# Two sums of weights made by transfers, and the tensor engine held in program order through the mixer's attention stage

## The chip, the cores and the metric

The kernel runs on one core of a Trainium2 chip. The metric is the device time of one execution in microseconds (us). The time before is 1540.34 us, the median of 3 runs (1540.05 to 1541.54). A profile is one execution, recorded instruction by instruction on the engines PE (matmul), DVE (vector), ACT (scalar), POOL (GpSimd) and SP (which only issues transfers).

## What is computed

Two layers of a decoder trunk on 512 tokens of width 1024, in float32. Each layer has three sub-layers with a norm before and after:

```python
def reference(x, mem, positions, rel_bias, ...):
    for l in range(DEPTH):                                   # 2
        a = hybrid_mixer(rms_norm(x, pre_mix_g[l]), ...)     # 8 latent heads and 8 dilated heads, one output projection
        x = x + rms_norm(a, post_mix_g[l])
        c = memory_cross_attention(rms_norm(x, pre_xattn_g[l]), rms_norm(mem, mem_g[l]), ...)   # 4 heads, 256 memory tokens
        x = x + rms_norm(c, post_xattn_g[l])
        hdn = jnp.square(jax.nn.relu(rms_norm(x, pre_mlp_g[l]) @ w_up[l]))      # width 4096
        x = x + rms_norm(hdn @ w_down[l], post_mlp_g[l])
    return x
```

In the mixer one input projection `w_in` gives the latent columns (query rank 384, key-value rank 256, 32 rotary) and the dilated heads' q, k, v. The latent heads get their queries and keys through a second, normalised projection. The dilated heads use a shared relative bias.

## The kernel before

**Precision.** Each float32 operand is split into a high and a low part, and each product is three matmuls: low by high, high by low, high by high (`mm`, L234, its matmuls at L240 to L242). Weights arrive by SP's queue in a `raw` buffer (8 of them, `raw_w`, L151); ACT writes the high part `whi` and DVE the low part `wlo` (`parts_w`, L161, without a gain; `load_w`, L168, with a gain per row at L192 and L198). There are five buffers each for high and low parts, and one comes free when PE has done the last product with it.

**Order.** A planner orders each engine's queue when the program is built: it goes by program order, and lifts an instruction ahead of others where, by its own model of times, its inputs are there and theirs are not. Two calls limit it. `tc.keep_in_program_order(ins)` keeps a PE instruction behind the PE instruction before it in the program. `tc.issue_after(ins)` queues what is in its block behind `ins` on that engine. Before the change the first call is used for transposes of some stages (`transpose`, L224, while `in_turn[0]` is set), the second for a few weight conversions.

**The mixer's stages.** First the dilated heads' v, q and k are projected (15 to 85.6 us in layer 0). `ev_kd` (L637) evicts each tile of k from PSUM: ACT writes `kh` (L642), DVE `kl` (L646), and POOL copies both to the other half of the partitions (L648). Then comes the attention stage (85.6 to 270.6 us in layer 0, 848.6 to 1027.4 in layer 1). `weave` takes steps in turn from the generator `attention()` and, as filling, from `latent()` (the latent projection, `ptm` with outputs `cq` and `ckv`; its transposes `ctp`; the second projections `pkn`, `pvm`; the queries' transposes `qtp`) and then `memory()` (the cross-attention's keys and values of the memory tokens: `pfm`, `ptm`). `attention()` makes for each of 16 heads four blocks of scores (`scores`, matmul `sp` at L470; DVE adds the bias and reduces at L474; ACT takes the exponential at L477; POOL normalises at L479), then for the head before it three groups of transposes (`ptp`, evicted by ACT at L498 and by DVE at L496), and for each pair of heads the weighted values (`op`, L231).

**PSUM.** There are four buffers of the products (`mm`), two of scores (`s`) and two of transposes (`t`). So the third score block of a head waits until DVE has read the first, and the third group of transposes until ACT has read the first.

**The MLP's second half.** The product with `w_down` is made in four quarters of the hidden width, each by seven products of half-size blocks instead of eight. The sums that these need are made on the activations in `left_forms` (L1018), and on the weights, in two groups g, in `right_form` (L1041) by DVE in place in the `raw` buffers: L1046 for product p = 5, L1048 for 6, L1050 for 7, L1052 for 4. `finish` (in the loop of products) adds each product into `acc` (L1120). After the last quarter, `done` (L1055) takes the sum of squares of a half row block (L373, the squares themselves go to a `junk` tile in SBUF), multiplies by the gain `gb` (L1058), and `add_post_norm` (L418) computes the scale (DVE `pnm` L421, POOL power `pnr` L139) and adds to the residual `xs` (L424). In layer 1 that result is transferred out; in layer 0 `norm_x` (L394) normalises it for the next layer (POOL L409 and ACT L406), and `transposed` makes the next layer's `xth` and `xtl`.

Of the kernel before, what the change touches and what calls it, by code (L numbers as in the profile page):

```python
# [45 lines left out]
def block_kernel(ctx: ExitStack, tc, x, mem, positions, rel_bias, w_in, q_norm_g, w_uq, kv_norm_g,  # L46
# [121 lines left out]
    def load_w(src, r0, kts, c0, width, gcol=None, heads=0):  # L168


        raw = raw_w(src, r0, kts, c0, width)
        hi = wp.tile([128, 2, 512], WD, tag="hi", name="whi")
        lo = wp.tile([128, 2, 512], WD, tag="lo", name="wlo") if SPLIT else None

        def cols(w, k, swap):
            v = w[:, k, :width]
            if not heads:
                return v
            if swap:
                return v.rearrange("p (h e c) -> p e h c", h=heads, e=2)  # L180
            return v.rearrange("p (e h c) -> p e h c", h=heads, e=2)

        if gcol is None and SPLIT:
            nc.scalar.activation(hi[:, :kts, :width], raw[:, :kts, :width], AF.Copy)  # L184
            nc.vector.tensor_sub(lo[:, :kts, :width], raw[:, :kts, :width], hi[:, :kts, :width].bitcast(F32))  # L185
            return hi, lo
        for k in range(kts):
            g = 1.0 if gcol is None else gT[:, gcol + k:gcol + k + 1]
            loads[0] += 1

            with tc.issue_after(token_parts[0]) if 3 <= loads[0] <= 8 else nullcontext():
# [31 lines left out]

    def transpose(out_, in_, ident_):  # L224
        ins = nc.tensor.transpose(out_, in_, ident_)  # L225
        if in_turn[0]:
            tc.keep_in_program_order(ins)
        clk[0] += 0.108

    def mm32(ps, lhsT, rhs, start, stop, rate=1.0):  # L230
        nc.tensor.matmul(ps, lhsT=lhsT, rhs=rhs, start=start, stop=stop)  # L231
        clk[0] += rhs.shape[-1] * 0.00167 * rate

    def mm(ps, lh, ll, rh, rl, first, last, more=False):  # L234
# [5 lines left out]
        nc.tensor.matmul(ps, lhsT=lh, rhs=rl, start=first, stop=False, skip_group_check=more)  # L240
        nc.tensor.matmul(ps, lhsT=ll, rhs=rh, start=False, stop=False, skip_group_check=more)  # L241
        nc.tensor.matmul(ps, lhsT=lh, rhs=rh, start=False, stop=last, skip_group_check=more)  # L242
# [127 lines left out]
    def sumsq(src, ss, scale=1.0):  # L370
        w = src.shape[-1]
        junk = unit("junk", (128, w))
        nc.scalar.activation(junk, src, AF.Square, scale=scale, accum_out=ss)  # L373
# [83 lines left out]
    behind = [None]  # L457

# [3 lines left out]
    def scores(P, parts, tb, scale):  # L462
# [3 lines left out]
        for i in range(NT):  # L466
            L = 128 * (i + 1)
            sp = pss.tile([128, 512], F32, tag="s", name="sp")
            for n, (q, k) in enumerate(parts):
                nc.tensor.matmul(sp[:, :L], lhsT=q[:, i * 128:(i + 1) * 128], rhs=k[:, :L],  # L470
                                 start=n == 0, stop=n == len(parts) - 1)
# [5 lines left out]
            nc.scalar.activation(Pi, Pi, AF.Exp, bias=nm[:, i:i + 1], scale=-1.0, accum_out=rs[:, i:i + 1])  # L477
# [89 lines left out]
    for l in range(DEPTH):  # L567
# [50 lines left out]
        def ev_ckv(t, ps):  # L618
            ckv[t] = unit("ckv")
# [17 lines left out]
        def ev_kd(m, ps):  # L637

            for a in range(2):
                here, there = slice(a * 64, a * 64 + 64), slice(64 - a * 64, 128 - a * 64)  # L640
                u = unit("kh", dt=WD)
                nc.scalar.activation(u[here, :], ps[here, :], AF.Copy)  # L642
# [240 lines left out]

        weave(attention(), [latent_gen, memory()], lambda: RATIOS[0] if not scored[0] else RATIOS[1])
        OTh = [o[0] for o in outs]
# [132 lines left out]
        def left_forms(F, ra, rb):  # L1018
# [11 lines left out]
            nc.vector.tensor_add(s1, a21, a22)  # L1030
            part(5, s1)
            nc.vector.tensor_sub(s2, s1, a11)
# [4 lines left out]
            nc.vector.tensor_sub(a12, a12, s2)  # L1037
# [3 lines left out]
        def right_form(p, b):  # L1041
# [3 lines left out]
            if p == 5:  # L1045
                nc.vector.tensor_sub(b11, b12, b11)  # L1046
            elif p == 6:
                nc.vector.tensor_sub(b11, b22, b11)  # L1048
            elif p == 7:
                nc.vector.tensor_sub(b12, b22, b12)  # L1050
            elif p == 4:
                nc.vector.tensor_sub(b11, b21, b11)  # L1052
            return parts_w({1: b11, 5: b11, 6: b11, 2: b21, 7: b12, 3: b22, 4: b11}[p])

        def done(t, n):  # L1055

            sumsq(acc[t][n], ss[t][:, n:n + 1], scale=1.0 / 32.0)
            nc.vector.tensor_mul(acc[t][n], acc[t][n], gb[n])  # L1058
            ready_halves[t] += 1
            if ready_halves[t] < 2:  # L1060
                return
# [7 lines left out]
        for qd_ in range(4):  # L1069
# [33 lines left out]
            for p, ps, first, last, dsts in plan:  # L1103
# [9 lines left out]
                def finish(j):  # L1113
                    for d, n in dsts:
                        t = d + j
                        if acc[t][n] is None:
                            acc[t][n] = unit("acc")
                            nc.vector.tensor_copy(acc[t][n], ps[j])  # L1118
                        else:
                            nc.vector.tensor_add(acc[t][n], ps[j], acc[t][n])  # L1120
                        if end and p in (2, 3, 4) or end and p == 7 and n == 1:
                            done(t, n)
# [9 lines left out]
                for g in range(2):  # L1132
                    w = right_form(p, B[g])
# [3 lines left out]
                if end and p == 7:  # L1137
                    last_w = [right_form(4, B[g]) for g in range(2)]
# [45 lines left out]
```

## Time and profile before

| | us |
|---|---|
| median of 3 runs | 1540.34 |
| runs from, to | 1540.05, 1541.54 |
| profiled execution, device time | 1542.4 |
| profiled execution, span | 1540.6 |
| PE busy in the span | 1504.2 |
| DVE, ACT, POOL busy in the span | 996.6, 820.6, 240.2 |

The span runs from the first to the last instruction of the profiled execution; that execution's device time is 1.8 us longer. In a timeline each row is a start, a duration, engine, line, operation, the tiles written and read, the shape, and in brackets the idle time before it with what ended it. Consecutive matmuls overlap in their modelled durations, so the pitch from start to start tells more than the duration. [...]

### The profile page before, as it was taken

Reading aid. Unit: us, or ns where it says so; the run is one execution under the profiler, and the core shown is the slowest. Engines: PE = TensorE matmul, PEld = TensorE weight load, DVE = VectorE, ACT = ScalarE, POOL = GpSimd, SP = SyncE. Lnnn points to the kernel's source line nnn. Section 1 sums busy time; section 2 is a strip of 40 time slices with the busy share of each in tenths; the row PEclk is TensorE's granted clock in tenths of the full one; section 3 lists DMA queues with packets and bytes.
Section 4 is the critical chain, followed back from the end, with each engine's and each line's share of the span. In section 5 each row is a group of like instructions: output and inputs, shape, how many; then the busy total and the mean of one; then the engine's idle time right before and its main releaser. Section 6 shows DMA issues by size and latency. Waiting matters only on the chain.

```text
span 1540.6 us, 21293 instructions
## 1 busy us (share of the span) xinstructions
PE 1504.2 (98%) x7861; PEld 1262.7 (82%) x7861; DVE 996.6 (65%) x1780; ACT 820.6 (53%) x1578; POOL 240.2 (16%) x429
## 2 busy tenths in 40 slices
PE   8999999999999999999989999999999999999996
PEld 6778788898898888888878877978988988888885
DVE  4556766456458668685974666654554695958678
ACT  5365666346456464544553666654454654546363
POOL 2053721021020000000012445201111100000001
PEclk9999999999999999999999999999999999999999
DMA  6423223513131505151542331253322324060612
GB/s 226 161 75 112 82 76 102 193 56 123 55 110 56 178 28 178 41 165 61 171 137 68 117 108 58 69 168 120 109 83 69 124 75 144 25 195 14 192 55 82
DMA packets 87404, 164.09 MB, mean 107 GB/s; under 512 B 6230, under 2 KB 12036, under 8 KB 87300
## 3 DMA queue, kind: packets, MB, share of 16 engines
q1 hardware_dynamic: 86724, 161.68, 32.3%
q8 instruction: 62, 1.02, 0.3%
q10 hardware_dynamic: 576, 1.05, 0.2%
q14 instruction: 42, 0.34, 0.1%
HBM read 154.29 MB, written 11.03 MB: 107 GB/s over the span
## 4 chain that ended last, share of the span: by engine, by line
PE 81%; DVE 8%; issue 6%; ACT 3%; POOL 1%; DMA 1%; SPq 0%; POOLq 0%; DVEq 0%; ACTq 0%
PE pfm L241 11%; PE pfm L240 11%; PE pfm L242 11%; PE ptm L240 6%; PE ptm L241 6%; PE ptm L242 6%; PE wa L240 3%; PE wa L242 3%; PE wa L241 3%; PE sp L470 3%; PE op L231 3%; PE ptp L225 2%; DVE wlo L198 2%; PE wc L240 2%; PE wc L242 2%
## 5 line engine op out<-in xcount | busy, mean ns | idle before, releaser
L241 PE MATMUL pfm<-xth,wlo 128*128 128x512 f32 (+1 forms) x896 | 322.4, 360 | 0.6
L240 PE MATMUL pfm<-xtl,whi 128*128 128x512 f32 (+1 forms) x896 | 322.2, 360 | 0.0
L242 PE MATMUL pfm<-xth,whi 128*128 128x512 f32 (+1 forms) x896 | 321.6, 359 | 0.0
L198 DVE SCALAR_TENSOR_TENSOR wlo<-raw,gT,whi 128x512 fp32r<-128x512 f32 (+3 forms) x332 | 229.6, 729 | 140.3 <-ACT whi L192 138.7
L192 ACT ACTIVATE whi<-raw,gT 128x512 fp32r<-128x512 f32 (+2 forms) x324 | 209.5, 697 | 187.6 <-PE pfm L242 100.3
L164 ACT ACTIVATE whi<-raw 128x1024 fp32r<-128x1024 f32 x112 | 118.1, 1060 | 143.0 <-PE pfm L242 52.8
L241 PEld LDWEIGHTS pfm<-xth,wlo 128*128 128x128 f32 x896 | 169.2, 189 | 27.2 <-DVE wlo L198 1.4
L242 PEld LDWEIGHTS pfm<-xth,whi 128*128 128x128 f32 x896 | 169.2, 189 | 25.5 <-issue 0.5
L240 PEld LDWEIGHTS pfm<-xtl,whi 128*128 128x128 f32 x896 | 169.2, 189 | 24.7
L165 DVE TENSOR_TENSOR wlo<-raw,whi 128x1024 fp32r<-128x1024 f32 x112 | 134.9, 1219 | 34.3 <-ACT whi L164 34.3
L139 POOL TENSOR_TENSOR pnr<-pnm,mhalf 128x1 f32<-128x1 f32 x24 | 18.0, 750 | 828.7 <-DVE pnm L421 828.6
L479 POOL TENSOR_SCALAR P<-P,rs 128x128 f32<-128x128 f32 (+3 forms) x128 | 72.0, 568 | 150.8 <-PE sp L470 66.3
L240 PE MATMUL wa<-wlo,fh 128*128 128x512 f32 x240 | 93.6, 390 | 0.5 <-DVE acc L1118 0.5
L241 PE MATMUL wa<-whi,fl 128*128 128x512 f32 x240 | 93.4, 389 | 0.0
L242 PE MATMUL wa<-whi,fh 128*128 128x512 f32 x240 | 93.4, 389 | 0.0
L477 ACT ACTIVATE P<-P,nm 128x128 f32<-128x128 f32 (+3 forms) x128 | 71.3, 558 | 23.4 <-DVE nm L474 22.8
L185 DVE TENSOR_TENSOR wlo<-raw,whi 128x1024 fp32r<-128x1024 f32 x32 | 39.1, 1222 | 59.3 <-ACT whi L184 58.6
L240 PE MATMUL ptm<-wlo,xth 128*128 128x512 f32 (+2 forms) x192 | 70.0, 365 | 3.9 <-DVE wlo L198 3.5
L184 ACT ACTIVATE whi<-raw 128x1024 fp32r<-128x1024 f32 x32 | 33.9, 1061 | 67.3 <-PE ptm L242 64.5
L241 PE MATMUL ptm<-whi,xtl 128*128 128x512 f32 (+2 forms) x192 | 67.7, 352 | 0.1
L242 PE MATMUL ptm<-whi,xth 128*128 128x512 f32 (+2 forms) x192 | 67.0, 350 | 0.0
L240 PEld LDWEIGHTS wa<-wlo,fh 128*128 128x128 f32 x240 | 45.0, 188 | 10.6 <-DVE acc L1118 1.4
(249 smaller groups left out, 3273.6 us busy)
## 6 DMA issues: line engine op xcount, KB each, us to landing
raw<-in_w_up SPq DMA_DIRECT2D x64, 512.0 KB, 4.6
raw<-in_w_down SPq DMA_DIRECT2D x64, 512.0 KB, 4.4
raw<-in_w_in SPq DMA_DIRECT2D x24, 512.0 KB, 5.7
raw<-in_w_xk SPq DMA_DIRECT2D x16, 512.0 KB, 4.4
raw<-in_w_xv SPq DMA_DIRECT2D x16, 512.0 KB, 3.7
raw<-in_w_mix_out SPq DMA_DIRECT2D x16, 512.0 KB, 4.4
raw<-in_w_xq SPq DMA_DIRECT2D x16, 512.0 KB, 5.4
raw<-in_w_xo SPq DMA_DIRECT2D x16, 512.0 KB, 3.5
```

The lines of the kernel that those rows point to most:

```text
L164: nc.scalar.activation(hi, raw, AF.Copy)
L165: nc.vector.tensor_sub(lo, raw, hi.bitcast(F32))
L185: nc.vector.tensor_sub(lo[:, :kts, :width], raw[:, :kts, :width], hi[:, :kts, :width].bitcast(F32))
L192: weight_parts[:] = [nc.scalar.activation(cols(hi, k, False), cols(raw, k, True), AF.Copy, scale=g).ins]
L198: nc.vector.scalar_tensor_tensor(lv, rv, g, hv, op0=OP.mult, op1=OP.subtract)
L231: nc.tensor.matmul(ps, lhsT=lhsT, rhs=rhs, start=start, stop=stop)
L240: nc.tensor.matmul(ps, lhsT=lh, rhs=rl, start=first, stop=False, skip_group_check=more)
L241: nc.tensor.matmul(ps, lhsT=ll, rhs=rh, start=False, stop=False, skip_group_check=more)
L242: nc.tensor.matmul(ps, lhsT=lh, rhs=rh, start=False, stop=last, skip_group_check=more)
L470: nc.tensor.matmul(sp[:, :L], lhsT=q[:, i * 128:(i + 1) * 128], rhs=k[:, :L], start=n == 0, stop=n == len(parts) - 1)
L477: nc.scalar.activation(Pi, Pi, AF.Exp, bias=nm[:, i:i + 1], scale=-1.0, accum_out=rs[:, i:i + 1])
L479: nc.gpsimd.tensor_scalar(Pi, Pi, rs[:, i:i + 1], 1.0, op0=OP.mult, op1=OP.mult)
```

## The change

Five edits, most of them in the two places named above.

1. The conversions of chunks 1 to 3 of the first latent load on ACT (rows `r0` not 0) are queued behind the third k tile's second `kh` eviction (`behind_keys`), until the first `ckv` is evicted. In the attention stage the first exponential of each head is queued behind the last `kh` eviction (`last_key`).
2. While `pinned` is set, which is through the whole `weave` of the attention stage in both layers, each PE matmul and transpose is kept in program order (`in_order`).
3. The sums of activations and weights change sign, so that all sums of weights are additions. In the last quarter of each layer the sums for p = 4 and p = 7 are no longer made by DVE: a transfer issued by GpSimd reads the second block from memory and adds it into the buffer (4 of 512 KB per layer, 8 in all). `finish` turns the sign of one half of the columns.
4. The junk squares of `done` go to a PSUM buffer of the pool `t`, but for p = 2.
5. In layer 1 the first two token tiles are finished by `finish_by_transfer`: DVE computes `acc` times scale times `gb` in one step, GpSimd issues a transfer that adds the residual from memory (4 of 256 KB), and SP transfers the result out. Their residual is no longer loaded.

```diff
-            with tc.issue_after(token_parts[0]) if 3 <= loads[0] <= 8 else nullcontext():
+            after = token_parts[0] if 3 <= loads[0] <= 8 else behind_keys[0] if r0 else None
+            with nullcontext() if after is None else tc.issue_after(after):
                 weight_parts[:] = [nc.scalar.activation(cols(hi, k, False), cols(raw, k, True), AF.Copy, scale=g).ins]
...
+    def in_order(ins):
+        if pinned[0]:
+            tc.keep_in_program_order(ins)
+
     def transpose(out_, in_, ident_):
         ins = nc.tensor.transpose(out_, in_, ident_)
         if in_turn[0]:
             tc.keep_in_program_order(ins)
+        else:
+            in_order(ins)
...
-        nc.tensor.matmul(ps, lhsT=lh, rhs=rl, start=first, stop=False, skip_group_check=more)
+        in_order(nc.tensor.matmul(ps, lhsT=lh, rhs=rl, start=first, stop=False, skip_group_check=more))
...
-            nc.scalar.activation(Pi, Pi, AF.Exp, bias=nm[:, i:i + 1], scale=-1.0, accum_out=rs[:, i:i + 1])
+            with tc.issue_after(last_key[0]) if pinned[0] and i == 0 else nullcontext():
+                nc.scalar.activation(Pi, Pi, AF.Exp, bias=nm[:, i:i + 1], scale=-1.0, accum_out=rs[:, i:i + 1])
...
-                nc.scalar.activation(u[here, :], ps[here, :], AF.Copy)
+                last_key[0] = nc.scalar.activation(u[here, :], ps[here, :], AF.Copy).ins
+                if m == 2 and a == 1:
+                    behind_keys[0] = last_key[0]
...
+        pinned[0] = True
         weave(attention(), [latent_gen, memory()], lambda: RATIOS[0] if not scored[0] else RATIOS[1])
+        pinned[0] = False
...
-            if p == 5:
-                nc.vector.tensor_sub(b11, b12, b11)
...
+            tile_, more, at = {1: (b11, None, None), 5: (b11, b12, None), 6: (b11, b22, None), 4: (b11, b21, (1, 0)),
+                               2: (b21, None, None), 7: (b12, b22, (1, 1)), 3: (b22, None, None)}[p]
+            if more is not None and at and qd_ == 3:
+                r0, c0 = qd_ * 1024 + g * 512 + at[0] * 256, at[1] * 512
+                nc.gpsimd.dma_start(tile_, w_down[l][r0:r0 + 256, c0:c0 + 512].rearrange("(k p) c -> p k c", p=128),
+                                    accum_op=OP.add)
+            elif more is not None:
+                nc.vector.tensor_add(tile_, tile_, more)
+            return parts_w(tile_)
+
+        def finish_by_transfer(t):
+            m = small("pnm", 1)
+            nc.vector.scalar_tensor_tensor(m, ss[t][:, 0:1], EPS, ss[t][:, 1:2], op0=OP.add, op1=OP.add)
+            r = rpow(m, "pn")
+            for n in range(2):
+                rows, cols = slice(t * 128, (t + 1) * 128), slice(n * 512, (n + 1) * 512)
+                nc.vector.scalar_tensor_tensor(acc[t][n], acc[t][n], r[:, 0:1], gb[n], op0=OP.mult, op1=OP.mult)
+                nc.gpsimd.dma_start(acc[t][n], xmid[rows, cols], accum_op=OP.add)
+                nc.sync.dma_start(out[0, rows, cols], acc[t][n])
...
-                            done(t, n)
+                            done(t, n, None if p == 2 else t_ps("junkp"))
...
-                        load_x(t, xmid)
+                        if l < DEPTH - 1 or t >= 2:
+                            load_x(t, xmid)
```

## Rows read from the trace of the kernel before

**Rows 1.** The page: busy time and instructions, and the granted clock by slice.
```profile
PE 1504.2 (98%) x7861; PEld 1262.7 (82%) x7861; DVE 996.6 (65%) x1780; ACT 820.6 (53%) x1578; POOL 240.2 (16%) x429
PEclk9999999999999999999999999999999999999999
```
**Rows 2.** Windows by stage: window, length, busy us of each engine, clock, DMA.
```profile
85.60:270.60 185.00, 176.05 (x1121) 147.58 (x1121) 123.48 (x349) 120.18 (x290) 77.15 (x148) 0.99 0.28 93
270.60:760.00 489.40, 488.83 (x2424) 413.96 (x2423) 319.23 (x442) 248.33 (x418) 31.21 (x48) 1.00 0.33 105
760.00:790.00 30.00, 25.79 (x110) 20.28 (x109) 27.75 (x48) 22.86 (x50) 9.58 (x12) 0.89 0.67 216
848.60:1027.40 178.80, 173.41 (x1121) 145.96 (x1121) 119.89 (x343) 115.66 (x283) 69.25 (x136) 1.00 0.30 97
```
**Rows 3.** Timeline of ACT and PE where layer 0's attention stage starts.
```profile
81.81 0.96 ACT L192 ACTIVATE whi<-raw,gT 128x288 fp32r<-128x288 f32 x2 [12.98 <-PE pfm L242]
...
87.03 0.59 ACT L642 ACTIVATE kh<-pfm 64x512 fp32r<-64x512 f32 x1
...
85.41 0.39 PE L242 MATMUL pfm<-xth,whi 128*128 128x512 f32 x1
88.44 0.50 PE L470 MATMUL sp<-kh,qs 128*128 128x128 f32 x2 [2.64 <-POOL kh L648]
```
**Rows 4.** Windows right after two waits of PE, columns as above.
```profile
88.50:92.70 4.20, 3.81 (x16) 3.36 (x17) 2.62 (x7) 3.22 (x5) 3.80 (x7) 0.60 0.14 52
...
775.00:779.00 4.00, 3.77 (x14) 3.09 (x14) 3.86 (x7) 4.00 (x11) 0.72 (x2) 0.57 0.00 0
```
**Rows 5.** Timeline: layer 1's start, and head 3's transposes in both layers.
```profile
844.74 0.59 ACT L642 ACTIVATE kh<-pfm 64x512 fp32r<-64x512 f32 x1 [0.75 <-DVE kl L646]
...
848.64 0.22 PE L470 MATMUL sp<-kh,qs 128*128 128x128 f32 x1
...
122.08 0.93 PE L225 MATMUL ptp<-ident,P 128*128 128x128 f32 x7
...
878.96 0.93 PE L225 MATMUL ptp<-ident,P 128*128 128x128 f32 x7
```
**Rows 6.** Timeline of DVE and PE at the step between the layers.
```profile
758.64 1.22 DVE L1052 TENSOR_TENSOR raw<-raw 128x1024 f32<-128x1024 f32 x1
...
763.25 1.22 DVE L1052 TENSOR_TENSOR raw<-raw 128x1024 f32<-128x1024 f32 x1
...
775.23 1.82 PE L225 MATMUL tp<-ident,xn 128*128 128x128 f32 x8 [2.38 <-POOL xn L409]
...
781.17 0.50 PE L240 MATMUL ptm<-wlo,xth 128*128 128x512 f32 x1 [1.84 <-DVE wlo L198]
```
**Rows 7.** DMA issues by tile: count, size, median us to landing.
```profile
raw<-in_w_down SPq DMA_DIRECT2D x64, 512.0 KB, 4.4
...
xs<-xmid SPq DMA_DIRECT2D x16, 256.0 KB, 2.7
```
**Rows 8.** Timeline of ACT, PE and DVE at the end.
```profile
1523.87 1.06 ACT L164 ACTIVATE whi<-raw 128x1024 fp32r<-128x1024 f32 x1 [4.83 <-DVE raw L1052]
...
1526.80 0.50 PE L240 MATMUL we<-wlo,fh 128*128 128x512 f32 x1 [1.08 <-DVE wlo L165]
...
1529.42 0.39 PE L242 MATMUL we<-whi,fh 128*128 128x512 f32 x1
...
1535.68 1.41 DVE L424 SCALAR_TENSOR_TENSOR xs<-acc,pnr,xs 128x512 f32<-128x512 f32 x2 [0.66 <-POOL pnr L139]
```
**Rows 9.** Timeline of PE in layer 0's attention stage, single places.
```profile
119.57 0.45 PE L470 MATMUL sp<-kh,qs 128*128 128x384 f32 x1 [0.49 <-DVE nm L474]
...
130.59 0.55 PE L225 MATMUL ptp<-ident,P 128*128 128x128 f32 x3
...
188.05 0.39 PE L240 MATMUL pkn<-cl,whi 128*128 128x512 f32 x1
...
216.41 0.33 PE L470 MATMUL sp<-ring 96*128 96x128 f32 x1 [0.20 <-ACT ring L202]
```

More of the change, by code (lines that the diff above doesn't have):

```diff
@@ L227, in transpose @@
             tc.keep_in_program_order(ins)
+        else:
+            in_order(ins)
         clk[0] += 0.108
     def mm32(ps, lhsT, rhs, start, stop, rate=1.0):
-        nc.tensor.matmul(ps, lhsT=lhsT, rhs=rhs, start=start, stop=stop)
+        in_order(nc.tensor.matmul(ps, lhsT=lhsT, rhs=rhs, start=start, stop=stop))
         clk[0] += rhs.shape[-1] * 0.00167 * rate
@@ L239, in mm @@
             return
-        nc.tensor.matmul(ps, lhsT=lh, rhs=rl, start=first, stop=False, skip_group_check=more)
-        nc.tensor.matmul(ps, lhsT=ll, rhs=rh, start=False, stop=False, skip_group_check=more)
-        nc.tensor.matmul(ps, lhsT=lh, rhs=rh, start=False, stop=last, skip_group_check=more)
+        in_order(nc.tensor.matmul(ps, lhsT=lh, rhs=rl, start=first, stop=False, skip_group_check=more))
+        in_order(nc.tensor.matmul(ps, lhsT=ll, rhs=rh, start=False, stop=False, skip_group_check=more))
+        in_order(nc.tensor.matmul(ps, lhsT=lh, rhs=rh, start=False, stop=last, skip_group_check=more))
     def chunks(src, r0, nk, c0, width, gcol, rot=0):
@@ L368, in feat_major, with sumsq @@
         run(feat_major_steps(*a, **k))
-    def sumsq(src, ss, scale=1.0):
+    def sumsq(src, ss, scale=1.0, junk=None):
         w = src.shape[-1]
-        junk = unit("junk", (128, w))
+        if junk is None:
+            junk = unit("junk", (128, w))
         nc.scalar.activation(junk, src, AF.Square, scale=scale, accum_out=ss)
@@ L457, in block_kernel @@
     behind = [None]
+    behind_keys = [None]
+    last_key = [None]
+    pinned = [False]
     def new_scores():
@@ L469, in scores @@
             for n, (q, k) in enumerate(parts):
-                nc.tensor.matmul(sp[:, :L], lhsT=q[:, i * 128:(i + 1) * 128], rhs=k[:, :L],
-                                 start=n == 0, stop=n == len(parts) - 1)
+                in_order(nc.tensor.matmul(sp[:, :L], lhsT=q[:, i * 128:(i + 1) * 128], rhs=k[:, :L],
+                                          start=n == 0, stop=n == len(parts) - 1))
                 clk[0] += L * (0.00042 if SPLIT else 0.00167)
@@ L618, in ev_ckv @@
         def ev_ckv(t, ps):
+            behind_keys[0] = None
             ckv[t] = unit("ckv")
@@ L1029, in left_forms @@
             part(1, a11)
-            nc.vector.tensor_add(s1, a21, a22)
+            nc.vector.tensor_sub(s1, a22, a21)
             part(5, s1)
-            nc.vector.tensor_sub(s2, s1, a11)
+            nc.vector.scalar_tensor_tensor(s2, s1, -1.0, a11, op0=OP.mult, op1=OP.subtract)
             part(6, s2)
@@ L1036, in left_forms, with right_form @@
             part(7, a21)
-            nc.vector.tensor_sub(a12, a12, s2)
+            nc.vector.scalar_tensor_tensor(a12, a12, -1.0, s2, op0=OP.mult, op1=OP.subtract)
             part(3, a12)
             part(4, a22)
-        def right_form(p, b):
+        def right_form(p, b, g):
             b11, b12, b21, b22 = b
-            if p == 5:
-                nc.vector.tensor_sub(b11, b12, b11)
[L1047 to L1053, printed above, removed]
@@ L1055, in done @@
-        def done(t, n):
-            sumsq(acc[t][n], ss[t][:, n:n + 1], scale=1.0 / 32.0)
-            nc.vector.tensor_mul(acc[t][n], acc[t][n], gb[n])
+            tile_, more, at = {1: (b11, None, None), 5: (b11, b12, None), 6: (b11, b22, None), 4: (b11, b21, (1, 0)),
[6 more added lines that the diff above has]
+                nc.vector.tensor_add(tile_, tile_, more)
@@ L1059, in done @@
+        def done(t, n, junk):
+            sumsq(acc[t][n], ss[t][:, n:n + 1], scale=1.0 / 32.0, junk=junk)
+            by_transfer = l == DEPTH - 1 and t < 2
+            if not by_transfer:
+                nc.vector.tensor_mul(acc[t][n], acc[t][n], gb[n])
             ready_halves[t] += 1
             if ready_halves[t] < 2:
+                return
+            if by_transfer:
+                finish_by_transfer(t)
                 return
@@ L1117, in finish @@
                             acc[t][n] = unit("acc")
-                            nc.vector.tensor_copy(acc[t][n], ps[j])
+                            nc.vector.tensor_scalar(acc[t][n], ps[j], (1.0, -1.0)[n], None, op0=OP.mult)
+                        elif n:
+                            nc.vector.tensor_sub(acc[t][n], acc[t][n], ps[j])
                         else:
@@ L1132, in block_kernel @@
                 for g in range(2):
-                    w = right_form(p, B[g])
+                    w = right_form(p, B[g], g)
                     for i in range(2):
@@ L1137, in block_kernel @@
                 if end and p == 7:
-                    last_w = [right_form(4, B[g]) for g in range(2)]
+                    last_w = [right_form(4, B[g], g) for g in range(2)]
                 if end and p == 1:
```

## The prediction

> **What bounds the kernel now.** I read the page first: the tensor engine (PE) is busy 1504.2 of 1540.6 us and the granted clock is near full everywhere [rows 1]. So 36 us at most are there to be had, and what matters is where they lie. The table by stage answers that [rows 2]: from 270.6 to 760 us PE is busy 488.83 of 489.40, so projections, cross-attention and most of the MLP have nothing to give. The losses are the attention stage of layer 0 (185.00 minus 176.05, 9.0 us) and of layer 1 (178.80 minus 173.41, 5.4 us), the step from layer 0 to 1 (30.00 minus 25.79, 4.2 us) and what follows the last matmul, which starts at 1529.42 in a span that ends at 1540.6 [rows 1, 8]. Both attention stages hold 1121 matmuls, so their difference is all waiting and clock. Busy time hides part of the loss: under half clock PE is busy but slow, so I also read the granted clock of short stretches [rows 4].
>
> **Start of the attention stage, layer 0 (edit: behind_keys, last_key).** The chain reads backwards: the first score `sp` begins at 88.44 after 2.64 us of waiting for POOL's copy of `kh`; POOL waited for ACT's `kh` eviction at 87.03; and ACT had been stuck until 81.81, 12.98 us idle, on a weight conversion whose buffer PE had not released, so that key evictions queued behind conversions nobody needed yet [rows 3]. After that idle PE ran at a granted clock of 0.60 over 88.5 to 92.7 [rows 4], the lower level for most of it. Layer 1 runs the same code with the keys ahead of the conversions: `kh` at 844.74, then `sp` at 848.64 with no wait [rows 5]. From the stage's start to the same transposes of head 3 it takes 122.08 minus 85.64 (the last `pfm` starts at 85.41 [rows 3], and one follows the next at 0.23), 36.44 us in layer 0, and 878.96 minus 848.64, 30.32 us in layer 1 [rows 5]. The edit puts chunks 1 to 3 of the first latent load behind the sixth key eviction, which is layer 1's order. So 6.1 us, and that also is the upper end; lower end 5.0 if the conversions, now later, make the first latent product wait about the 0.96 us that one takes [rows 3]. What queues behind a waiting conversion on ACT is the next evictions, which is why it must stand behind keys. I take **−6.1**.
>
> **Layer boundary (edit: sums by transfer, junk in PSUM).** In the last quarter DVE is the engine that is late: PE waits 2.38 us at 775.23 and 1.84 us at 781.17 [rows 6], and the clock is 0.57 over 775 to 779 [rows 4]. That lost about (1 − 0.57) × 4.0 = 1.7 us more; if the second wait cost the same clock again, it is some 7.6 us together. Ahead of these waits in DVE's queue stand L1052's sums for p = 4, at 758.64 and 763.25, 1.22 us each [rows 6], and the sums of p = 7 earlier still. Taking two of them out moves DVE's queue up by 2 × 1.22 = 2.4 us, which covers the first wait and its clock drop (2.38 + 1.7 = 4.1), and part of the second. The Square of an accumulator no longer needs a unit of its own, which costs nothing and gains nothing that a row shows. I take **−5**; the ends are −1.5 (POOL's two small steps, not DVE, set `xn`) and −8 (both waits and both drops gone). What is late next would be POOL's `xn` scaling, which the row names as releaser.
>
> The sums themselves go to transfers of 512 KB issued by POOL, of a kind that no row here shows. Nearest: the plain 512 KB loads, 4.4 us to landing, and 256 KB loads, 2.7 us [rows 7]. The p = 7 pair has its buffers free a quarter of the stage before its parts are wanted. For p = 4 a transfer can start once p = 6's parts have been split, which stands ahead of 758.64 in DVE's queue, and its own parts are split after 763.25 now [rows 6]: issued by about 755, and with 4.4 us, it lands before DVE would have begun the second sum. So I cost them at nothing on PE; were they over 12 us, PE would wait in the last product. POOL has nothing queued behind them but the 0.55 us powers. SP's queue keeps only loads. The changed signs replace adds one for one; `tensor_scalar` for `tensor_copy` likewise: 0, within ±0.3.
>
> [...] First the row: DVE's sums of 128x1024 take 1.22 us, and DVE is nearly without a gap there [rows 6]. [...]
>
> **Tail (finish_by_transfer, sums).** The last conversion of weights on ACT starts at 1523.87 after 4.83 us of waiting for the p = 4 sum; PE waits 1.08 us at 1526.80 for DVE's half of it; the last `xs` is at 1535.68 and the span ends 1540.6 [rows 8]. In the change two sums (2.4 us) and four multiplications (four times 0.6) leave DVE. PE's wait goes: 1.1. After the last matmul (1529.42) DVE still had a backlog; without it: last add about 1529.4 (the matmul comes 1.1 earlier too), sum of squares 0.85, power 0.8, two `xs` steps 1.41 [rows 8], then 3.6 us for the transfer out as now: end near 1537.3. **−3.3**, ends −1.0 (only the PE wait) and −4.1. Tokens 0 to 255 get a transfer of their own after the `xs` step; they are ready some 15 us before the end, against 2.7 us [rows 7] for a plain 256 KB, so they stay hidden up to about 10 us.
>
> **The pinned order (in_order).** This is the only term that costs. Without it the planner lifts ready products in front of a matmul or transpose that would wait. With it PE stands still in each such wait and does the lifted products afterwards. A step of the latent projection is 12 products in the program; where the trace shows it cut, for example 2 products, scores, then 10, products were lifted. The lift is worth their pitch only if the wait was real, and it was: at nearly every cut the next group starts within 0.1 us of its releaser. Per layer (layer 1 repeats layer 0), with a pitch of 0.174 us for 384 columns, 0.131 for 288, 0.227 for 512, 0.118 for 256:
> - Scores. The third score of a head needs the buffer of the first, hence DVE's reduction. At 119.57 three products had been lifted (0.52) and 0.49 us was still left to wait [rows 9]; at the next head two had been (0.35). Heads 0 and 1, with up to ten lifted: 1.1 to 1.6; the rest: 1.05.
> - Transposes of P. The third group waits for ACT's copy of the first (two buffers): two products lifted before 130.59 [rows 9], 0.35 each, twice here; near 242.6 four of 0.118, near 256 four of 0.227: 2.1 in all.
> - The latent transposes, 139 to 152: ten cut products: 1.2.
> - 161 to 184: DVE sets the pace there, lifted work only moves: 0 (−0.5 to +1.3).
> - 184.7 to 203: six products `pkn` from 188.05 on stand in front of a transpose that still waited for DVE's `mtl` [rows 9]: 6 × 0.23 = 1.4.
> - The queries' transposes, 212 to 218.5: the score at 216.41 waits for ACT's and DVE's eviction of the transposes (0.54 + 0.68 after them) [rows 9]; eleven products of 0.118 and a group of transposes lifted: 2.2.
> - Three small places: 0.5.
> Sum about 9 per layer, **+18** for both. From above 24: each lift in full, and two waits of over 2 us that bring the half clock, since after waits of 2.64 and 2.38 us the clock fell here [rows 3, 4, 6]. From below 12: one wait lets DVE and ACT catch up, so the next is shorter. At most, if most lifts only trade one wait for another, 5 to 8.
>
> **Sum.** −6.1 − 5 − 3.3 + 18 = +3.6 (3.5 with rounding) on the profiled execution of 1542.4 us: 1545.9. The median of the runs is 1540.34, 2.06 less: **1543.8**.
>
> **Rivals.**
> - *The pin is half price* (the catch-up above; every engine behind PE also has slack: DVE 65%, ACT 53% [rows 1]). Then 9 in place of 18: 1534.8, faster. For it: the two stages lose 9.0 and 5.4 us even with the lifts [rows 2], so lifted work does not fill every wait. Against: the rows of release.
> - *The gains come half, the pin in full.* In layer 0 the pinned scores of head 0 wait on the same keys [rows 3]; at the boundary POOL's steps decide. −7 + 18 = +11 on the forecast's basis, 1551. Slower; decides where the boundary keeps both waits of 775.23 and 781.17 [rows 6].
> [...]
> - *It does little*: buffer releases hold the old order in place, and keys stay late. 1540.
> - *Program order is better than the planner's*, since a lifted group of transposes can also block the buffer that a score's transposes need: pin 0, 1526.
>
> **How the numbers follow.** Measurement can tell 0.2%, 3.1 us, from no change. Forecast 0.40 (0.27 of it slower, 0.13 within); half price 0.30 (0.27 faster, 0.03 within); gains by half 0.12, slower; starved 0.05 (0.04 slower, 0.01 within); does little 0.08, within; program order better 0.05, faster. Faster 0.32, same 0.25, slower 0.43. The range goes from below half price, 1532, to 1553; the likeliest case by itself, 1538 to 1550 (pin 12 to 24).
>
> **What would show it.** Layer 0's first `sp` without the 2.64 us and the clock of 88.5 to 92.7 at 1.00: first term right. PE's busy time from 760 to 790 near 30: second. No wait before the last `we`: third. In both attention stages the steps of 12 uncut, with idle time of PE up by 6 to 12 us per stage: the pin's price; if that idle time is up by under 5, the forecast fails on the fast side. [...]

## The result, and the profile after

The changed kernel takes 1583.91 us (median of 4 runs, 1579.58 to 1586.9) against 1540.94 of the kernel before: a ratio of 1.0275, 95% interval 1.0262 to 1.0287. It is 43 us slower; I had forecast 3.5 us slower and a range that ended at 1553. The sign was right, the size was wrong by a factor of twelve. The profile below is of the longest of the four executions (1586.9 us).

The two attention stages of the kernel after, from the first score on, as windows (columns as in rows 2: window, length, busy us and count of PE, PEld, DVE, ACT and POOL, granted TensorE clock with 1.00 for the full one, DMA share, GB/s):

```profile
84.06:291.40 207.34, 183.21 (x1121) 156.08 (x1120) 125.87 (x350) 120.39 (x291) 72.56 (x140) 0.93 0.27 84
869.60:1073.30 203.70, 181.10 (x1123) 154.49 (x1122) 122.14 (x344) 116.87 (x285) 68.79 (x136) 0.94 0.26 85
```

Against [rows 2] two things grew for the same 1121 matmuls. PE's idle time in layer 1 went from 5.4 to 22.6 us, in layer 0 from 9.0 to 24.1. And PE's busy time grew by 7.7 us in layer 1 and 7.2 in layer 0, with the mean clock down from 1.00 to 0.94 and from 0.99 to 0.93. So of some 47 us in the two stages 32 are waits and 15 are clock, in this execution; its mean clock was 0.978, that of the shortest of the four (1579.58 us) 0.985. Outside the stages nothing moved by more than 1.6 us. The 1.6 us by which the first stage starts earlier are not the edits' doing: it starts 2.1 us earlier in the trace of the pin by itself and 2.2 in that of the MLP's edits by themselves (both below), which have no edit in common.

What PE waits for, summed over the whole execution (columns: us in total, times, longest), in the kernel before:

```profile
PE sp L470 <- DVE nm L474: 4.5, 10, 0.8
PE tp L225 <- POOL xn L409: 3.7, 2, 2.4
```

The same view of the kernel after:

```profile
PE sp L481 <- DVE nm L485: 18.3, 19, 2.9
PE ptp L230 <- ACT PT L510: 5.0, 10, 0.7
PE ptm L247 <- DVE wlo L199: 4.6, 3, 2.9
PE tp L230 <- POOL xn L417: 4.0, 2, 2.7
```

The score that waits for DVE's reduction went from 4.5 to 18.3 us. The last line, which belongs to the step between the layers, did not go away.

**Layer 0's start.** A timeline of PE, ACT and DVE in the kernel after, which answers [rows 3]:

```profile
84.06 0.22 PE L481 MATMUL sp<-kh,qs 128*128 128x128 f32 x1
...
88.12 0.40 PE L247 MATMUL ptm<-wlo,xth 128*128 128x288 f32 x1 [2.89 <-DVE wlo L199]
...
86.20 0.59 ACT L655 ACTIVATE kh<-pfm 64x512 fp32r<-64x512 f32 x1 [6.79 <-DVE kl L661]
86.82 0.53 ACT L193 ACTIVATE whi<-raw,gT 128x288 fp32r<-128x288 f32 x1
...
84.43 0.29 DVE L485 CUSTOM_DVE_ANT_0 P<-sp,tb 128x128 f32<-128x128 f32 x1 [9.68 <-PE sp L481]
...
84.76 1.41 DVE L661 TENSOR_TENSOR kl<-pfm,kh 64x512 fp32r<-64x512 f32 x2
```

The first score no longer waits (2.64 us before). But DVE stood idle for 9.68 us ahead of a score reduction that waited for PE's score, with the low halves of the keys queued behind that reduction; ACT's next key eviction waited 6.79 us for those, the weight conversion stood behind that eviction as the edit wants it, and PE waited 2.89 us for the weights. The wait went from the score to the product behind it. The window after it has a granted clock of 0.57, as against 0.60 behind the score's wait in [rows 4] (second line: the stretch after another pinned wait, in layer 1):

```profile
88.00:96.00 8.00, 7.40 (x28) 6.32 (x28) 5.90 (x19) 6.77 (x16) 5.67 (x8) 0.57 0.38 99
964.00:972.00 8.00, 7.43 (x32) 7.13 (x33) 5.05 (x19) 3.18 (x10) 3.30 (x7) 0.66 0.02 5
```

**A pinned wait.** PE and DVE in layer 1, the timeline around the longest wait of this kind:

```profile
950.33 0.44 PE L481 MATMUL sp<-kh,qs 128*128 128x384 f32 x1 [1.69 <-DVE nm L485]
...
964.57 1.33 PE L481 MATMUL sp<-ring 96*128 96x384 f32 x3 [2.85 <-DVE nm L485]
...
962.76 0.88 DVE L833 TENSOR_SCALAR mr<-mr,nmr 128x512 f32<-128x512 f32 x2 [0.68 <-POOL nmr L139]
963.56 0.68 DVE L205 TENSOR_TENSOR ring<-qtp,ring 96x512 fp32r<-96x512 f32 x1
964.16 0.15 DVE L385 SCALAR_TENSOR_TENSOR nmm<-mms 128x1 f32<-128x1 f32 x1
964.23 0.28 DVE L485 CUSTOM_DVE_ANT_0 P<-sp,mask 128x128 f32<-128x128 f32 x1
```

PE's third score block waits for DVE's reduction of the first, and DVE has steps of the memory tokens' norm (`mr`, `nmm`) and an eviction (`ring`) in its queue ahead of that reduction. In the kernel before, the longest wait of this kind was 0.8 us; here PE stands for 2.85.

**The step between the layers and the end.** The timeline of PE at the step between the layers, which answers [rows 6]:

```profile
792.06 0.39 PE L249 MATMUL we<-whi,fh 128*128 128x512 f32 x1
795.15 1.84 PE L230 MATMUL tp<-ident,xn 128*128 128x128 f32 x8 [2.70 <-POOL xn L417]
...
799.68 1.08 PE L230 MATMUL tp<-ident,xn 128*128 128x128 f32 x4 [2.06 <-DVE xtl L205]
```

The timeline of PE's last matmul and of DVE at the end, which answers [rows 8]:

```profile
1574.13 0.39 PE L249 MATMUL we<-whi,fh 128*128 128x512 f32 x1
...
1575.90 0.69 DVE L1089 TENSOR_TENSOR acc<-acc,gb 128x512 f32<-128x512 f32 x1 [0.85 <-ACT junkp L381]
...
1576.58 0.68 DVE L1156 TENSOR_TENSOR acc<-we,acc 128x512 f32<-128x512 f32 x1
...
1580.09 1.42 DVE L432 SCALAR_TENSOR_TENSOR xs<-acc,pnr,xs 128x512 f32<-128x512 f32 x2 [0.66 <-POOL pnr L139]
```

The step between the layers has its two waits as before, 2.70 and 2.06 us for 2.38 and 1.84. At the end PE's last wait of 1.08 us is gone, but from the last matmul to the span's end it takes 1585.1 − 1574.1 = 11.0 us, for 1540.6 − 1529.4 = 11.2.

The transfers that add (DMA issues: count, KB, median us to landing) land in time:

```profile
raw<-in_w_down POOLq DMA_DIRECT2D x8, 512.0 KB, 6.0
acc<-xmid POOLq DMA_DIRECT2D x4, 256.0 KB, 4.9
```

### The profile page after: what moved, and what is told of

Same layout as the page of the kernel before. It is cut to its first block, busy times and chain, and to the rows that moved or that the text cites. A ratio compares the mean times of both kernels' runs of the same rounds, so it can differ in the third digit from the quotient of the medians.

```text
span 1585.1 us, 21307 instructions
## 1 busy us (share of the span) xinstructions
PE 1517.7 (96%) x7861; PEld 1279.5 (81%) x7861; DVE 988.6 (62%) x1768; ACT 822.7 (52%) x1578; POOL 252.5 (16%) x441
## 3 DMA queue, kind: packets, MB, share of 16 engines
q8 instruction: 62, 1.02, 0.3%
## 4 chain that ended last, share of the span: by engine, by line
PE 82%; DVE 9%; ACT 3%; issue 3%; POOL 2%; DMA 1%; SPq 0%; DVEq 0%; POOLq 0%; ACTq 0%
PE pfm L247 12%; PE pfm L248 12%; PE pfm L249 12%; PE ptm L247 7%; PE ptm L248 7%; PE ptm L249 7%; PE sp L481 3%; PE wa L247 3%; PE wa L249 3%; PE wa L248 3%; PE op L238 2%; DVE wlo L199 2%; PE ptp L230 2%; PE wc L249 1%; PE wc L248 1%
## 5 line engine op out<-in xcount | busy, mean ns | idle before, releaser
L165 DVE TENSOR_TENSOR wlo<-raw,whi 128x1024 fp32r<-128x1024 f32 x112 | 134.7, 1219 | 39.5 <-ACT whi L164 39.5
L1067 POOL DMA_DIRECT2D raw<-in_w_down x8 | 9.8, 1230 | 596.3 <-DVE raw L1070 540.1
L1070 DVE TENSOR_TENSOR raw<-raw 128x1024 f32<-128x1024 f32 x56 | 67.9, 1217 | 0.2
```

The source lines that it names most:

```text
L165: nc.vector.tensor_sub(lo, raw, hi.bitcast(F32))
L1070: nc.vector.tensor_add(tile_, tile_, more)
```

## The experiments

Theory A: the pin is the whole loss, since no product may fill a wait any more, and the clock that falls behind such waits (0.57 over 88 to 96, behind 2.89 us) is part of it. Rivals: the order forced on ACT makes a good part of it (B); the pinned order of scores and transposes among themselves does (C). Each ratio below is to the kernel before in the same set of runs.

**The pin by itself.** Every matmul and transpose of the attention stage goes through `in_order`; nothing else is changed.

```diff
+    def in_order(ins):
+        if pinned[0]:
+            tc.keep_in_program_order(ins)
...
```

> The kernel before with nothing but the pinned order of the attention stage. Theory A (the pin is the whole loss): the stage of layer 1 takes about 24 us more, as in the changed kernel (203.7 for 178.8), and layer 0's too, in all 1540.5 + 45 to 50, about 1587. Theory B (the order of the keys and of the exponentials makes a good part of it, since it holds ACT): clearly less, under 1570.

Measured: 1586.0 us, ratio 1.0295 (1.0279 to 1.031), 46 us more. The pin alone costs all of the loss. Theory B falls.

**Everything but the pin.**

```diff
     def in_order(ins):
-        if pinned[0]:
-            tc.keep_in_program_order(ins)
+        return
```

> The changed kernel with the pin alone taken out (exponentials still behind the keys, conversions behind the keys, sums by transfer). Theory A: the attention stages return to 179 and 185 or less, the start of layer 0's stage gains 2 to 6, the tail 1.5, the boundary nothing: 1532 to 1539. Theory B: the stages stay long, over 1555.

Measured: 1536.39 us, ratio 0.9974 (0.9964 to 0.9984), 3.7 us faster than before. With the pin the same edits stand at 1583.91: 47.5 us between them.

**The order of the keys by itself.**

```diff
+            after = token_parts[0] if 3 <= loads[0] <= 8 else behind_keys[0] if r0 else None
...
+            with tc.issue_after(last_key[0]) if pinned[0] and i == 0 else nullcontext():
```

> The kernel before with nothing but the conversions and first exponentials queued behind the key evictions. If the order of ACT sets layer 0's start, as I forecast, it gains the 6.1 us: 1534. Rival: DVE's queue also holds a score reduction ahead of the low halves of the keys, so keys stay late and the gain is 0 to 2, 1539 to 1541.

Measured: 1537.28 us, ratio 0.9979 (0.997 to 0.9988), 2.8 us faster. Neither number was met: more than the rival's 0 to 2, under half of the 6.1 that I forecast. In its trace the first score starts at 83.78, but DVE's reductions still stand ahead of the low halves.

**The edits of the MLP by themselves.** Changed sums, signs, junk squares and finish; neither the pin nor the order of the keys.

```diff
-            with tc.issue_after(last_key[0]) if pinned[0] and i == 0 else nullcontext():
...
```

> The kernel before with nothing but the edits of the MLP: changed signs, two sums by transfer, junk squares in PSUM, two tiles finished by transfer. From the changed kernel's trace, where the step between the layers lost as much as before and the tail gained 1.6 us: 1539 (1537 to 1541). My forecast's terms (5 and 3.3) would give 1532.

Measured: 1539.54 us, ratio 0.9994 (0.9985 to 1.0003): no change that can be told, as the first number said. My two terms had promised 8.3 us.

**Products free, the rest pinned.** All three matmuls of `mm` are left free.

```diff
-        in_order(nc.tensor.matmul(ps, lhsT=lh, rhs=rl, start=first, stop=False, skip_group_check=more))
+        nc.tensor.matmul(ps, lhsT=lh, rhs=rl, start=first, stop=False, skip_group_check=more)
...
```

> The changed kernel with the three matmuls of each split product left free; scores, transposes and weighted values stay pinned. Theory A (the loss is that no product fills a wait): the attention stages come back to about 180 us each, the whole to 1536 to 1542, as without the pin. Rival (the pinned order of the scores and transposes among themselves is what holds PE up): it stays over 1555.

Measured: 1544.46 us, ratio 1.0024 (1.0015 to 1.0034). Windows of its two stages:

```profile
84.17:270.51 186.34, 175.05 (x1122) 146.47 (x1121) 124.78 (x351) 119.83 (x291) 74.37 (x140) 0.98 0.29 93
848.43:1032.11 183.68, 173.26 (x1123) 145.88 (x1121) 120.70 (x344) 116.06 (x283) 70.58 (x136) 0.99 0.29 95
```

Of the 47.5 us, 39.5 come back when only the products may be lifted; the order of scores, transposes and weighted values accounts for the 8 us that stay (1544.46 − 1536.39), 2.5 over the upper end of A's expectation. So A holds for the main part and C for the rest. One thing no run separates: the planner orders the other engines' queues too, and pinning PE changed those. In layer 0's stage some 50 of DVE's 350 instructions stand at another place in the changed kernel's trace than in that of the run without the pin. How much of the 39.5 us is PE standing still by itself, and how much the other queues' new order, is open.

**The waits filled with work on zeros.**

```diff
+            if pinned[0] and i == 2:
+                idle_products(8)
             sp = pss.tile([128, 512], F32, tag="s", name="sp")
```

> The changed kernel with eight small products of zeros, in program order, ahead of the third score block of each head, where PE waits for DVE's reduction. They do no work of the reference's. If the clock is a loss of its own, about 7.5 us in each attention stage as PE's longer busy time there shows: in the stage the granted clock of the stretches after these waits comes back near 1.00; against that stand up to 0.9 us per head where there was no wait so long. Expected 1572 to 1582 if the clock counts by itself. If the clock falls for another reason than the waits ahead of it, its drops stay and the time goes up by 10 to 25 us, to 1594 or more.

Measured: 1592.49 us, ratio 1.0322 (1.0304 to 1.0341): 8.6 us above the changed kernel, so the saving that I expected did not come. Its trace is of an execution of 1586.62 us, 5.6 us under the other three (1592.18 to 1592.88), so it may flatter. Windows of it behind four of the places in layer 1 and one in layer 0; the changed kernel has 0.72 over 926 to 938, 0.79 over 950 to 958 and 0.59 over 1014 to 1022:

```profile
930.00:938.00 8.00, 6.66 (x46) 5.70 (x45) 5.76 (x15) 4.22 (x11) 3.15 (x6) 1.00 0.35 116
950.00:958.00 8.00, 6.55 (x49) 5.64 (x48) 7.03 (x22) 5.83 (x15) 3.74 (x7) 1.00 0.36 119
1014.00:1022.00 8.00, 6.80 (x55) 6.64 (x56) 5.33 (x13) 5.70 (x12) 0.86 (x2) 1.00 0.25 75
962.00:970.00 8.00, 5.55 (x24) 5.16 (x25) 5.67 (x20) 4.13 (x13) 3.21 (x6) 0.79 0.12 47
87.00:95.00 8.00, 6.80 (x36) 5.54 (x36) 6.15 (x19) 7.09 (x16) 5.74 (x8) 0.79 0.33 90
```

Three of layer 1's four drops are gone, though most of the waits ahead of the last of them remained; the fourth, behind a wait that the idle products do not fill, stayed (0.79 over 962 to 970), and so did four of five in layer 0 (0.79 over 87 to 95, 0.68 over 151 to 155, 0.66 over 183 to 187, 0.63 over 231 to 235). That idle work holds the clock does not follow: two of the three drops are also missing in runs that have the same waits and no idle work. Below are PE's timeline ahead of the drop at 926 to 938 in the changed kernel, then the same waits in the run with the pin by itself, with the window behind them as its last line:

```profile
922.81 0.44 PE L481 MATMUL sp<-kh,qs 128*128 128x384 f32 x1 [0.66 <-DVE nm L485]
...
925.80 0.55 PE L230 MATMUL ptp<-ident,P 128*128 128x128 f32 x3 [1.04 <-DVE cl L205]
926.86 0.66 PE L230 MATMUL ctp<-ident,ckv 128*128 128x128 f32 x4 [0.51 <-ACT PT L510]
...
928.92 1.11 PE L230 MATMUL ctp<-ident,cq 128*128 128x128 f32 x4 [0.98 <-DVE cl L205]
```

```profile
925.57 0.44 PE L477 MATMUL sp<-kh,qs 128*128 128x384 f32 x1 [0.66 <-DVE nm L481]
...
928.57 0.55 PE L229 MATMUL ptp<-ident,P 128*128 128x128 f32 x3 [1.03 <-DVE cl L204]
929.62 0.66 PE L229 MATMUL ctp<-ident,ckv 128*128 128x128 f32 x4 [0.51 <-ACT PT L505]
...
931.69 0.66 PE L229 MATMUL ctp<-ident,cq 128*128 128x128 f32 x4 [0.98 <-DVE cl L204]
...
928.70:940.70 12.00, 9.93 (x65) 8.55 (x66) 9.15 (x24) 7.13 (x18) 6.57 (x14) 1.00 0.36 112
```

The run with the low halves first (next) has the waits ahead of the drop at 1014 to 1022 (0.99, 0.44 and 1.35 us) and a clock of 1.00 over 1006 to 1014 behind them. The third, at 950, is missing where the wait ahead of it is shorter (0.48 us for 1.69), in one execution. So this run does not show the clock's part of the loss, which is read from the busy time, as time to be had: by the median the idle work cost 8.6 us more than it saved.

**The low halves of the keys ahead of DVE's first reduction.**

```diff
+            with tc.issue_after(last_low[0]) if pinned[0] and i == 0 else nullcontext():
...
```

> The changed kernel with the first score reduction of each head queued on DVE behind the low halves of the keys. If DVE's reduction ahead of the low halves is what kept ACT's keys and then the first latent product late at layer 0's start: PE's wait of 2.89 us there goes, with the clock drop behind it, 4 to 6 us, about 1579. If the weights themselves are late, nothing: 1584.

Measured: 1578.43 us, ratio 1.0244 (1.0227 to 1.0261), 5.5 us faster than the changed kernel, whose interval begins at 1.0262. PE's wait for the weights at that place is 0.48 us in its trace, for 2.89, so the chain read above, reduction ahead of low halves ahead of keys ahead of weights, is shown for that wait. Where the 5.5 us come from is not. PE waits 1.02 and 0.94 us for score reductions right behind instead, the clock behind them is still down (0.57 over 88 to 96; from 90.25 on the products of 288 columns start every 0.24 us, for 0.13 from 84.34 on), and over the two stages PE's idle time is 47.1 us, for 46.7. The two traces' stages differ in PE's busy time, 9 us less, with a mean clock of 0.989 for 0.978 in one execution of each.

**The memory norm earlier.**

```diff
-MEM_AT = 30
+MEM_AT = 12
```

> The changed kernel with the norm of the memory tokens taken up after 12 steps of the latent projection in place of 30, so that DVE's steps for it do not stand ahead of a latent head's score reduction. If the wait of PE for that reduction (2.5 to 3.0 us in each layer) came from what stood ahead in DVE's queue: that wait goes, with its clock drop, 6 to 10 us in both layers, about 1576. If it came from PE's own order: the same, 1584.

Measured: 1580.14 us, ratio 1.0251 (1.0236 to 1.0267), 3.8 us faster, less than 6 to 10, and the intervals overlap a little (the changed kernel's begins at 1.0262). In its trace the wait of 2.85 us is gone, but the score that now meets the norm in DVE's queue waits longer (1.70 us at 919.05; the same score waits 0.66 us in the changed kernel, at 922.81), and layer 1's stage got only 1 us shorter, layer 0's 4. What stood in the queue was the cause of that wait; in a pinned order much of it comes back at another.

**Three buffers of scores.**

```diff
-    psm = ctx.enter_context(tc.tile_pool(name="psm", bufs=4, space=bass.MemoryType.PSUM))
-    pss = ctx.enter_context(tc.tile_pool(name="pss", bufs=2, space=bass.MemoryType.PSUM))
+    psm = ctx.enter_context(tc.tile_pool(name="psm", bufs=3, space=bass.MemoryType.PSUM))
+    pss = ctx.enter_context(tc.tile_pool(name="pss", bufs=3, space=bass.MemoryType.PSUM))
```

> The changed kernel, pinned, with three PSUM buffers of scores in place of two, and three of products in place of four. If PE's waits in pinned order come mostly from the third score block waiting for the first's buffer (18.3 us of waits behind DVE's reduction in the changed kernel, and the clock drops behind them): 12 to 20 us faster than it, about 1568. If DVE is late there whatever the buffers, the waits move to the fourth block and the transposes: within 4 us of 1584.

Measured: 1573.51 us, ratio 1.0213 (1.0198 to 1.0227), 10.4 us faster than the changed kernel, just short of what the first theory wanted. PE's waits in its trace:

```profile
PE ptp L230 <- ACT PT L510: 9.0, 12, 2.0
...
PE sp L481 <- DVE nm L485: 3.7, 8, 0.7
```

The score's wait fell by 14.6 us, the transposes' wait for ACT's copies rose by 4.0. The run also takes a buffer from the products, and that has a price outside the two stages: in its trace the stages are 12.6 and 7.3 us shorter than the changed kernel's, while the step between the layers takes 3.6 us more, the stretch from the first attention stage to that step 2.9 and what follows the second stage 1.8. Both theories have a part: the buffer is a real cause, worth more inside the stages than the 10.4 us, and a pinned queue passes some of a removed wait on to the next. PE's idle time in the stages fell by 8.7 us, not by 14.6.

**The pin only until the latent heads.** `unpin` is set when a layer's first latent head is scored and taken back in the next layer.

```diff
+                    unpin[0] = True
                     while min(keyed[0], queried[0]) <= i - 8:
```

> The changed kernel with the pin only until the first latent head is scored. If the loss is spread as the changed kernel's trace has it, with some 8 of 24 us per layer up to there: 1536 + 16 = 1552 (1548 to 1558). If the pinned first half leaves its delay to be caught up in the free second half: under 1545.

Measured: 1555.36 us, ratio 1.0096 (1.0081 to 1.0112): 19 us above the run without the pin. The free second half catches nothing up.

**The best of it, and the transfers once more.** First the order of keys and low halves without the pin:

> The changed kernel without the pin and with DVE's first score reduction of each head behind the low halves of the keys. If what was left of the loss at layer 0's start without the pin is DVE's reductions ahead of the low halves: 1 to 3 us under the run without the pin, 1533.5 to 1535.5. If the weights are late there anyway: the same 1536.4.

Measured: 1535.12 us, ratio 0.996 (0.9947 to 0.9972), 5.9 us faster than the kernel before; with the next one it is the fastest here. From the run without the pin (0.9964 to 0.9984) its interval does not part it. Then the same with `qd_ == 3` made never true, so that DVE makes all sums:

> The same as no_pin_low_first, but all sums of weights made by DVE again. If the transfers bring what I forecast at the boundary and the tail (a part of 8 us): 4 to 8 us slower than it. If the boundary hangs on the chain of norms behind the last product, and the tail gained only PE's last wait: 0.5 to 2 us slower.

Measured: 1535.05 us, ratio 0.9959 (0.9946 to 0.9971). The eight transfers in place of eight DVE sums show no gain: 4 to 8 us are excluded, the lower end of 0.5 is not, since each interval reaches some 2 us to either side.

## Why the prediction was wrong, step by step

**The pin, forecast +18, measured +46.** The mechanism was the one I named: lifted products fill waits, and the run with free products gives back 39.5 of 47.5 us. The sum of its terms failed. As listed they already add up to 9.6 to 10.1 us per layer, not 9; and the sign that I had named, idle time of PE up by 6 to 12 us per stage, came out at 15.2 and 17.2. From the start times of equally numbered matmuls in the two traces, layer 0's stage of the changed kernel, with each stretch given by its times in the kernel before (the clock's part included):

| stretch before, us | lost in the changed kernel | my term for it |
|---|---|---|
| 88 to 97 (start, one product behind it) | +2.4 | −6.1, in another term |
| 97 to 129 | −0.1 | 1.1 and part of 1.05 and 0.7 |
| 129 to 147 | +2.2 | 1.2 and the rest of these |
| 147 to 182 | +8.1 | 0 (−0.5 to +1.3) |
| 182 to 213 | +2.7 | 1.4 |
| 213 to 226 | +5.4 | 2.2 |
| 226 to 276 | +1.7 | 1.4 of the transposes' 2.1 |

The first step that failed is "161 to 184: DVE sets the pace there, lifted work only moves: 0". I argued that where DVE is the late engine, PE's order cannot matter. Here it was the other way round: where DVE was late, PE had long waits to fill (1.68 us at 168.32 and 2.30 at 182.03 in the kernel after), and the lifted products are work that PE needs no DVE for. Of the 8.1 us, 4.0 are idle time of PE (5.35 us there, for 1.34) and the rest its longer busy time at a clock of 0.84. The rows at 950.33 and 964.57 are of that stretch in layer 1.

The second is the clock. I named it only for the upper end of 24 (two waits of over 2 us), and took none into the 18. Layer 0's stage had five drops and layer 1's four, 15 us in all by PE's busy time, each down to 0.50. Several came behind a row of shorter waits rather than one long one, as the one over 151 to 153 behind 0.65, 1.04, 0.51, 0.98 and 0.58 us (141.72 to 149.55).

The third is method, and only argued: I priced a lift by the products that had been lifted, their count by their pitch. That is what the lift had been worth, not the length of the wait. In the kernel before a wait was filled and the queue went on; pinned, PE waits all of it, and what PE would have fed to DVE and ACT in that time is late as well. What is shown is that the catch-up that I allowed as the lower end (one wait makes the next one shorter) has its reverse: with the low halves first, the wait of 2.89 us went and PE's idle time in the stages stayed (47.1 us for 46.7).

**Layer 0's start, forecast −6.1 (−6.1 to −5).** The reading of ACT's queue was right, the size was not: 2.8 us alone, and in the changed kernel nothing, the pinned stretch from 88 to 97 even longer by 2.4. The step that failed is that the edit puts the conversions behind the keys, "which is layer 1's order", and so is worth the whole 6.1 us: it does so on ACT alone. I had not read DVE's queue, where the first reduction stands ahead of the low halves; [rows 3] are of ACT and PE only. In the pinned order that is what keeps PE waiting for its weights. Without the pin it is not what is missing: from the stage's beginning the matmuls come 3.1 us earlier than before with the order of the keys alone, 3.1 in the run without the pin, and 3.3 with the low halves first as well (from 2.6 us ahead at the stage's beginning to 5.9). So half of the 6.1 us was not this order. In the run without the pin layer 0 reaches the 106th matmul behind its first score after 18.3 us and layer 1 after 15.7; from there to the 200th both take 15.1. The rest lies in those first 106 matmuls; its cause I did not find.

**The step between the layers, forecast −5, measured +0.8 (−0.7 without the pin).** The step that failed is "Taking two of them out moves DVE's queue up by 2 × 1.22 = 2.4 us, which covers the first wait". My lower end named the reason for that wait, "POOL's two small steps, not DVE, set `xn`", and so the row has it. Ahead of it stands a chain: DVE's add, ACT's squares, DVE's `pnm`, POOL's power, DVE's `xs`, squares again, `n1m`, power, `xn`. The second wait ends with DVE's `xtl`, behind `pnm`, POOL's power and `xs` of the next tiles. The clock is 0.54 over 795 to 799, for 0.57 in [rows 4]. Taking 1.22 us steps out of DVE's queue shortened a queue that was not what PE waited for: the direct test gave 0.07 us between sums by DVE and by transfer, within a noise of some 2 us.

**The tail, forecast −3.3 (−4.1 to −1.0).** The first half, PE's wait of 1.08 us, is gone. The backlog behind the last matmul is not: the multiplication at 1575.90 waited 0.85 us for ACT's squares, and the last sum, ready earlier, stood behind it in DVE's queue. So 11.0 us for 11.2. The sum for this term had a wrong reading besides: the 1.41 us of `xs` in [rows 8] are both steps together, so its terms end at 1536.1 and not at 1537.3. And the PE wait went without the transfers of the sums too: in the run with all sums on DVE the last matmul starts within 0.1 us of the run with transfers. What is left for it is the rest of the MLP's edits, of which the four multiplications and the loads less of `finish_by_transfer` are the likeliest; I have not run that edit by itself, so this is not shown.

**Right.** The transfers were costed at nothing: they took 6.0 us to landing (5.7 to 7.4) for 4.4 of plain loads, under the 12 that I had set as the mark, and the one issued at 765.88 landed after 7.38 us in which DVE was busy throughout. No run shows a ground for the 0.05 that the forecast gives to "starved"; what the runs show in its place is these times to landing, 7.4 us at most. The rivals "half price", "does little" and "program order is better" fall with the pin alone at 1586; "gains by half" has its premise right at the boundary, which kept both waits, and at the keys with the wait moved to the product behind the score, but not its price.

## What to carry to other kernels

Before pinning an engine that is at 98%, list its waits as they would be with nothing to fill them, and price each at its full length with the clock behind it (15 of some 47 us here, in one execution); the products that a planner had lifted are only the part that it found. The order forced on ACT brought the weights to PE in time only when DVE's queue agreed (PE's wait of 2.89 us is 0.48 with the low halves first): read the queue of each engine that feeds the chain, here DVE's as well as ACT's. And work taken from a busy engine gained nothing here (0.07 us between sums by DVE and by transfer, within some 2 us) while the next engine waited for the end of a chain rather than for that engine's throughput.

## What the runs showed of the hardware that I had not expected

The granted clock fell to 0.50 not only after single waits of over 2 us, as over 89 to 95 after one of 2.89: it is 0.50 over 929 to 935 too, 0.72 over 926 to 938, after waits of PE of 0.66, 1.04, 0.51 and 0.98 us (922.81 to 928.92), and the transposes between them did not prevent it. Nor do the waits alone decide: the same matmuls with waits of 0.66, 1.03, 0.51 and 0.98 us left it at 1.00 in the run with the pin by itself. What decides that stays open, and one trace per kernel is little to price a drop from. The adding transfers of 512 KB took 6.0 us to landing (5.7 to 7.4) and held POOL 1.2 us each for their issue (1.19 to 1.40), with DVE busy beside them (8.00 us of 764 to 772).
